# One context round of the layer-1 feed-forward layer is recorded behind the experts' last weight load instead of ahead of it

## The chip, the cores and the metric

The kernel runs on one core of a Trainium2 chip. TensorE (PE) multiplies, VectorE (DVE), ScalarE (ACT) and GpSimd (POOL) do the elementwise work, and SyncE (SP) issues nearly all loads from the chip's memory (HBM). The metric is device time in microseconds. Half a per cent of it, 13 us, is about what a measurement of this kernel can tell from no change.

## The reference, cut to what matters

Two transformer blocks run one after the other on a sequence of 256 tokens, D = 1024. The first has attention, cross attention and a mixture of 32 experts whose weights are all read. The second has two layers, and in it a second sequence, the context, runs beside the tokens with the same weights until layer 1's keys and values:

```
x = first_block(x, ...)                # ends with _hier_moe(...), 32 experts
h, hc = x, ctx                         # second_block, for layer in range(2):
h  = h  + 0.5 * mod[:, 2]  * _swiglu(_modulate(h,  ...), ffn_w_in[layer, 0], ffn_w_out[layer, 0])
hc = hc + 0.5 * modc[:, 2] * _swiglu(_modulate(hc, ...), ffn_w_in[layer, 0], ffn_w_out[layer, 0])
nx = _modulate(h, ...); nc = _modulate(hc, ...)   # then the mixer of the layer
# in layer 1 (odd) the context gives only keys and values: kc, vc = split(nc @ w_qkv[:, qdim:])
```

_swiglu has an inner width of 2816, that is 22 blocks of 128. The context does not depend on the first block at all, so its work can run at any time ahead of layer 1's attention.

## The kernel before, in words

There are two streams of recorded instructions. The fore stream is the first block and then the tokens; its tiles have names that begin with f (fraw is a loaded weight tile of 1 MB, fsph and fspl its two split parts, fps a result in PSUM). The back stream is the context; its tiles begin with b (braw is a weight tile of half a megabyte, then bsph, bspl, bps). Each product in the split form takes three matmuls of 256 columns. The fore stream has three fraw buffers (`FORE`), the back stream four braw buffers (`BACK`). A scheduler merges the two streams by priorities (`SEG`), and within a stream each engine keeps the recorded order. All loads of both streams go through one queue, SP's, in one order.

A feed-forward layer (`ffn_steps`) is a generator that yields after each of six rounds (`ROUNDS`: blocks 0 and 1, then five rounds of four). A middle round computes the gate and up products of four blocks (8 braw loads, 4 x 48 matmuls) and the down products of four (4 braw loads, 96 matmuls): 12 loads and 288 matmuls.

The experts (`moe`) are eight groups of four. A group takes 16 loads of up and gate weights (w_eg, w_eu) and 8 of down weights (w_ed), 1 MB each, and a load feeds 4 matmuls of 128x32 tiles, which the trace counts as 8; four transposes stand between the two halves, and 8 matmuls at the end (16 in the trace) add the group's result into xres (`combine`). `moe_load` is the last of these loads. A loop for rare overflow follows, and then two normalizations, which are mostly DVE work, ahead of the tokens' layer 0. The generator c1a is the context's feed-forward layer of layer 1. The table `PLAN` says where its rounds are recorded: key -1 with the context's other work, which the scheduler may put among the experts; key 0 behind the experts, with loads behind `moe_load`; keys 6 and 8 at later steps of the tokens. The lines that do it:

```
        X = K.modulated(back, c, 1, 0, 1)
        K.c1a = K.ffn_steps(back, c, X, 1, 0, K.mods_col(1, 2, 1))
        late(PLAN.get(-1, ""))
...
            if w == "r":
                next(K.c1a)
...
            if i == 0:
                K.after["sync"] = K.moe_load
                back.seg(*SEG["c1a"])
            late(PLAN[i])
```

Of the kernel before, what the change touches and what calls it, by code (L numbers as in the profile page):

```python
# [1782 lines left out]

SPILL = 4
DEFER = 0
PLAN = {-1: 'rrr', 0: 'r', 6: 'r', 8: 'raak'}
PLAN_N = 32
CUT = ((0, 9, 9, 9, 9), (0, 3, 3, 3, 3))
FORE = dict(raw=3, sph=3, spl=3, xh=1, xl=1, k1=6, k2=4, k4=6, c=16, q1=4, dg=2, ld=1, dst=6, wg=2, gc=5, c72=1, rope=1)
# [6 lines left out]
def kernel(ctx: ExitStack, tc: tile.TileContext, I, out, dbg=None, stop=None):  # L1796
# [7 lines left out]
    def context():  # L1804
# [28 lines left out]
        K.nada = CUT[1][-1]  # L1833
        late(PLAN.get(-1, ""))
        if dbg:
            dbg("hc0c", c)

    def late(what):
        c = K.cres
        for w in what:  # L1840
            if w == "r":
                next(K.c1a)
            elif w == "a":
                m = K.nada
                K.nada += 1
                for _ in K.ada(back, 1, range(m, m + 1), ("raw",)):
                    pass
            elif w == "k":
                assert next(K.c1a, None) is None and K.nada >= 5
                if dbg:  # L1850
                    dbg("hc1a", c)
                K.odd_kv(back, K.modulated(back, c, 1, 3, 1))
# [49 lines left out]
    for i in range(PLAN_N):  # L1902
        if i in PLAN:
            K.cur, K.stream = back.chain, back
# [3 lines left out]
            elif "tensor" in fore.chain:  # L1908
                K.after["tensor"] = fore.chain["tensor"]
            late(PLAN[i])  # L1910
        K.cur, K.stream = fore.chain, fore
# [157 lines left out]
```

## Time and profile before

| | us |
|---|---|
| runs | 2605.69, 2612.25, 2616.22; median 2612.25 |
| profiled execution | 2622.72 |
| its span, first to last instruction | 2620.9 |
| chain that ended last | PE 38% of the span, DVE 6%, ACT 2%, DMA 1% |

The span is cut into stretches in what follows. The experts' stage lies between about 455 and 1350 us, the tokens' layer-0 feed-forward layer between about 1400 and 1600 us. Matmuls overlap, so busy time of PE says that it has work, and the count of matmuls in a stretch says how fast it goes through it.

### The profile page before, as it was taken

How to read it: one execution, taken by the hardware profiler on the slowest of the kernel's cores; microseconds unless marked ns; L12 is line 12 of the kernel's file. 1: busy time of each engine (PE TensorE's matmuls, PEld its weight loads, DVE VectorE, ACT ScalarE, POOL GpSimd, SP SyncE). 2: the span in 40 equal slices, each digit the busy share in tenths (PEclk: the TensorE clock that was granted, in tenths of full speed). 3: DMA queues.
4: the chain of work that ended last, by engine and by line, in shares of the span. 5: the costliest groups of instructions: out<-in, count | busy, mean ns of one | idle time of the engine just before them, and what ended most of it. 6: DMA issues, size and time to landing. Idle time of an engine off the chain costs nothing. (4 is left out here: it accounts for less than half of the span.)

```text
span 2620.9 us, 48434 instructions
## 1 busy us (share of the span) xinstructions
PE 2439.5 (93%) x19032; PEld 2075.9 (79%) x19032; DVE 1448.7 (55%) x3125; ACT 1187.1 (45%) x2342; POOL 731.1 (28%) x584
## 2 busy tenths in 40 slices
PE   6999998999989999999869999999999999889998
PEld 4767998786656788778439998888899899757998
DVE  6544667224432433243128667666767876667766
ACT  4433554334433343344225555455555555465554
POOL 1000145664424465646323004232000100424000
PEclk9999999999989999999869999999999999899999
DMA  9887443998988898989874554453455455355453
GB/s 340 325 318 249 165 146 113 344 333 319 345 320 324 329 347 290 362 322 349 316 295 169 190 181 160 148 193 125 150 191 181 158 180 183 113 187 193 163 187 118
DMA packets 115238, 617.37 MB, mean 236 GB/s; under 512 B 13232, under 2 KB 14704, under 8 KB 63936
## 3 DMA queue, kind: packets, MB, share of 16 engines
q1 hardware_dynamic: 113616, 610.20, 64.1%
q0 software_dynamic: 1392, 4.06, 0.5%
q8 instruction: 150, 2.46, 0.4%
q14 instruction: 80, 0.66, 0.1%
HBM read 612.11 MB, written 2.10 MB: 234 GB/s over the span
## 5 line engine op out<-in xcount | busy, mean ns | idle before, releaser
L58 POOL TENSOR_TENSOR bspl<-braw,bsph 128x512 fp32r<-128x512 f32 x468 | 609.4, 1310 | 919.1 <-ACT bsph L58 796.8
L58 ACT ACTIVATE fsph<-fraw 128x512 fp32r<-128x512 f32 x764 | 477.7, 628 | 524.7 <-PE fps L58 438.5
L58 DVE TENSOR_TENSOR fspl<-fraw,fsph 128x512 fp32r<-128x512 f32 x712 | 500.3, 706 | 299.7 <-ACT fsph L58 292.9
L58 PE MATMUL fps<-fxh,fsph 128*128 128x256 f32 (+1 forms) x2000 | 575.7, 288 | 3.7 <-ACT fxh L58 2.4
L58 PE MATMUL fps<-fxh,fspl 128*128 128x256 f32 (+1 forms) x2000 | 574.9, 287 | 3.3 <-POOL fspl L58 2.3
L58 PE MATMUL fps<-fxl,fsph 128*128 128x256 f32 (+1 forms) x2000 | 570.1, 285 | 6.6 <-DVE fxl L58 6.6
L58 ACT ACTIVATE bsph<-braw 128x512 fp32r<-128x512 f32 x468 | 291.6, 629 | 406.8 <-PE bps L58 353.9
L58 PEld LDWEIGHTS fps<-fxh,fsph 128*128 128x128 f32 x2000 | 385.1, 193 | 11.7 <-ACT fxh L58 4.1
L58 PEld LDWEIGHTS fps<-fxl,fsph 128*128 128x128 f32 x2000 | 384.7, 192 | 9.3 <-DVE fxl L58 8.9
L58 PEld LDWEIGHTS fps<-fxh,fspl 128*128 128x128 f32 x2000 | 383.9, 192 | 8.9 <-DVE fspl L58 4.5
L58 PE MATMUL bps<-bxh,bspl 128*128 128x256 f32 x1264 | 371.1, 294 | 2.2 <-ACT fk L58 2.2
L58 PE MATMUL bps<-bxh,bsph 128*128 128x256 f32 x1264 | 367.3, 291 | 5.2 <-ACT bsph L58 1.9
L58 PE MATMUL bps<-bxl,bsph 128*128 128x256 f32 x1264 | 364.0, 288 | 1.3 <-DVE bxl L58 1.3
L58 PE MATMUL fps<-fk,fsph 128*128 128x256 f32 x1632 | 298.9, 284 | 1.8 <-ACT fk L58 1.1
L58 PEld LDWEIGHTS bps<-bxh,bspl 128*128 128x128 f32 x1264 | 246.5, 195 | 53.4 <-POOL bspl L58 33.5
L58 PE MATMUL fps<-fraw,fk 128*32 128x512 f32 (+1 forms) x1600 | 235.9, 662 | 34.4 <-DMA fraw<-in_w_eu_dram 12.5
L58 PEld LDWEIGHTS bps<-bxh,bsph 128*128 128x128 f32 x1264 | 246.6, 195 | 26.6 <-issue 10.3
L58 PEld LDWEIGHTS bps<-bxl,bsph 128*128 128x128 f32 x1264 | 246.5, 195 | 17.8 <-issue 12.6
L58 PEld LDWEIGHTS fps<-fk,fsph 128*128 128x128 f32 x1632 | 254.8, 192 | 6.1 <-DVE fk L58 2.4
L58 POOL TENSOR_TENSOR fk<-fk,fk 128x512 f32<-128x512 f32 x16 | 21.6, 1352 | 768.1 <-ACT fk L58 763.0
L58 PE MATMUL fps<-fk,fspl 128*128 128x256 f32 x816 | 231.3, 283 | 0.0
L58 DVE SCALAR_TENSOR_TENSOR bk<-bk,bps 128x256 f32<-128x256 f32 (+1 forms) x148 | 60.5, 412 | 270.4 <-ACT bk L58 268.4
(357 smaller groups left out, 3465.7 us busy)
## 6 DMA issues: line engine op xcount, KB each, us to landing
fraw<-in_ffn_in_dram SPq DMA_DIRECT2D x88, 1024.0 KB, 4.9
braw<-in_ffn_in_dram SPq DMA_DIRECT2D x132, 512.0 KB, 6.2
fraw<-in_w_eg_dram SPq DMA_DIRECT2D x66, 1024.0 KB, 7.5
fraw<-in_w_eu_dram SPq DMA_DIRECT2D x66, 1024.0 KB, 7.5
fraw<-in_w_ed_dram SPq DMA_DIRECT2D x66, 1024.0 KB, 7.4
fraw<-in_ffn_out_dram SPq DMA_DIRECT2D x44, 1024.0 KB, 4.9
braw<-in_ffn_out_dram SPq DMA_DIRECT2D x66, 512.0 KB, 6.1
braw<-in_ada_w_dram SPq DMA_DIRECT2D x59, 512.0 KB, 6.6
```

The source lines that it names most:

```text
L58: r = f(*args, **kw)
```

## The change

One number in `PLAN` moves: of the layer's six rounds, three were recorded with the context and one at key 0; now it is two and two.

```
-PLAN = {-1: 'rrr', 0: 'r', 6: 'r', 8: 'raak'}
+PLAN = {-1: 'rr', 0: 'rr', 6: 'r', 8: 'raak'}
```

SP's queue in the seventh group of experts, before: the braw rows of ffn_in and ffn_out are the context's loads, the fraw rows are the experts'.

```order
L58 DMA braw_8412<-in_ffn_out_dram 128x1024
L58 DMA braw_8484<-in_ffn_in_dram 128x1024
L58 DMA fraw_13778<-in_w_eu_dram 128x2048
L58 DMA braw_8486<-in_ffn_in_dram 128x1024
L58 DMA fraw_13798<-in_w_ed_dram 128x2048
L58 DMA braw_8561<-in_ffn_in_dram 128x1024
L58 DMA fraw_13804<-in_w_ed_dram 128x2048
L58 DMA braw_8563<-in_ffn_in_dram 128x1024
L58 DMA braw_8639<-in_ffn_in_dram 128x1024
L58 DMA fraw_13810<-in_w_ed_dram 128x2048
```

The same place of SP's queue after the change, from the same first load on.

```order
L58 DMA braw_8412<-in_ffn_out_dram 128x1024
L58 DMA fraw_13320<-in_w_eu_dram 128x2048
L58 DMA fraw_13340<-in_w_ed_dram 128x2048
L58 DMA fraw_13346<-in_w_ed_dram 128x2048
L58 DMA fraw_13352<-in_w_ed_dram 128x2048
```

Twelve braw loads are gone from here; the experts' loads follow each other, 33 of them from this place to `moe_load`, where before 24 stood behind the last braw load. Ahead of this place the queue is the same.

PE's queue in the tokens' layer-0 feed-forward layer, before, somewhat behind its start: matmuls of the tokens alone.

```order
L58 MATMUL fps_14957<-fxh_14770,fspl_14991 128x256
L58 MATMUL fps_14957<-fxh_14770,fsph_15006 128x256
L58 MATMUL fps_14957<-fxl_14771,fsph_15006 128x256
L58 MATMUL fps_14957<-fxh_14770,fspl_15007 128x256
L58 MATMUL fps_14957<-fxh_14770,fsph_15006 128x256
L58 MATMUL fps_14957<-fxl_14771,fsph_15006 128x256
```

The same matmuls of the tokens after the change, with the context's (bps) between them.

```order
L58 MATMUL bps_14294<-bxh_7679,bsph_14327 128x256
L58 MATMUL fps_14957<-fxh_14770,fsph_15006 128x256
L58 MATMUL fps_14957<-fxl_14771,fsph_15006 128x256
L58 MATMUL bps_14294<-bxl_7680,bsph_14327 128x256
L58 MATMUL bps_14294<-bxh_7679,bspl_14328 128x256
L58 MATMUL bps_14294<-bxh_7679,bsph_14327 128x256
L58 MATMUL bps_14294<-bxl_7680,bsph_14327 128x256
L58 MATMUL bps_14294<-bxh_7679,bspl_14328 128x256
L58 MATMUL fps_14957<-fxh_14770,fspl_15007 128x256
```

The context's matmuls stand in groups of mostly one to seven along the whole layer, 288 in all, and the 12 loads stand among its weight loads. What follows the last expert load directly keeps its order on PE and SP: one round fills that place as before (it is the third round now, and the fourth is the one that stands in the tokens' layer). The rounds at keys 6 and 8 stay where they were.

## Rows read from the trace of the kernel before

**Rows 1.** The page: busy time, share of the span and instructions of each engine.

```profile
PE 2439.5 (93%) x19032; PEld 2075.9 (79%) x19032; DVE 1448.7 (55%) x3125; ACT 1187.1 (45%) x2342; POOL 731.1 (28%) x584
```

**Rows 2.** Stretches: length; busy (count) PE, PEld, DVE, ACT, POOL; clock, DMA share, GB/s.

```profile
1217.00:1260.00 43.00, 43.00 (x345) 34.25 (x344) 11.93 (x26) 17.63 (x32) 28.22 (x23) 1.00 0.92 344
...
1283.00:1325.00 42.00, 25.19 (x120) 2.79 (x114) 1.52 (x3) 0.60 (x1) 0.00 (x0) 0.60 0.96 359
...
1217.00:1283.00 66.00, 66.00 (x518) 52.81 (x520) 18.96 (x40) 24.58 (x44) 39.71 (x31) 1.00 0.84 309
1283.00:1350.00 67.00, 38.94 (x188) 5.20 (x182) 3.58 (x8) 1.96 (x4) 0.00 (x0) 0.62 0.93 348
1407.00:1597.00 190.00, 190.00 (x1604) 190.00 (x1603) 132.77 (x248) 101.94 (x183) 8.16 (x7) 1.00 0.53 187
1600.00:1700.00 100.00, 93.83 (x634) 83.75 (x633) 67.68 (x148) 49.67 (x101) 32.72 (x25) 0.95 0.42 147
```

**Rows 3.** Time line of SP's queue: start, length, load issued.

```profile
1215.63 0.33 SPq L58 DMA_DIRECT2D braw<-in_ffn_out_dram  x1
...
1218.92 0.33 SPq L58 DMA_DIRECT2D fraw<-in_w_eu_dram  x1
...
1224.42 0.33 SPq L58 DMA_DIRECT2D fraw<-in_w_ed_dram  x1
...
1228.48 0.33 SPq L58 DMA_DIRECT2D fraw<-in_w_ed_dram  x1
...
1261.25 0.33 SPq L58 DMA_DIRECT2D braw<-in_ffn_out_dram  x1
1264.53 0.33 SPq L58 DMA_DIRECT2D fraw<-in_w_eg_dram  x1
...
1283.98 0.33 SPq L58 DMA_DIRECT2D fraw<-in_w_eg_dram  x1
...
1317.47 23.73 SPq L58 DMA_DIRECT2D fraw<-in_w_ed_dram  x8
```

**Rows 4.** Time line of PE: start, length, matmuls, and in brackets the idle time before.

```profile
1217.79 1.07 PE L58 MATMUL fps<-fraw,fk 128*32 128x512 f32 x8
...
1223.29 1.07 PE L58 MATMUL fps<-fraw,fk 128*32 128x512 f32 x8
...
1227.35 1.07 PE L58 MATMUL fps<-fraw,fk 128*32 128x512 f32 x8
...
1323.02 1.94 PE L58 MATMUL fps<-fraw,fk 128*32 128x512 f32 x8 [1.20 <-DMA fraw<-in_w_eu_dram]
1325.76 1.12 PE L58 MATMUL fps<-consts,fk 128*128 128x128 f32 x4 [0.81 <-DVE fc L58]
1327.56 3.64 PE L58 MATMUL fps<-fraw,fk 128*32 128x512 f32 x16 [0.69 <-ACT fk L58]
...
1350.42 3.32 PE L58 MATMUL fps<-fk,fk 128*128 128x256 f32 x8
...
1353.81 1.89 PE L58 MATMUL fps<-fk,fk 128*128 128x256 f32 x8
```

**Rows 5.** The loads: issues, KB each, median us from issue to landing.

```profile
braw<-in_ffn_in_dram SPq DMA_DIRECT2D x132, 512.0 KB, 6.2
fraw<-in_w_eg_dram SPq DMA_DIRECT2D x66, 1024.0 KB, 7.5
```

**Rows 6.** The chain that ended last, where the tokens' layer begins: start, length, what.

```profile
1407.34 72.75 PE fps L58 x613
```

**Rows 7.** PE's waits between 1590 and 1900 us: total, times, longest.

```profile
PE fps L58 <- DVE fk L58: 11.3, 6, 3.9
PE bps L58 <- DMA braw<-in_ada_w_dram: 4.1, 3, 2.8
```

## The prediction

> **What bounds the kernel now.** I read the page first: PE is busy 93% of the span [rows 1]. That is an average over stages with different limits, so I cut the span into stretches around the change [rows 2], then read the queue of loads and PE's time line there [rows 3, 4], and the chain that ended last where the round arrives [rows 6].
>
> Three stretches matter. From 1217 to 1283 us PE is busy 66.00 of 66 us: the context's matmuls stand between the experts'. The loads are near their limit too, 344 GB/s up to 1260 us, and fall to 309 GB/s over the whole stretch, because PE still works off context matmuls while the experts' loads wait for their three buffers. From 1283 to 1350 us the context's work has run out. PE is busy 38.94 of 67 us, the granted clock is at its lower level most of the time (0.62 on average), and the loads bring 348 GB/s: here the loads alone set the pace. From 1407 to 1597 us, in the tokens' layer, it is the reverse: PE is busy 190.00 of 190 us at full clock, the loads have a share of 0.53, and the chain of work that ended last runs for 72.75 us over PE without a break [rows 6]. So the change takes a round out of a stage where bytes set the end and puts it into one where matmuls set it.
>
> **What it adds.** A round is 288 matmuls of 256 columns. In the tokens' layer 1604 matmuls take 190 us [rows 2], 0.1185 us each, and PE has no idle time there that could take them: 288 x 0.1185 = 34.1 us. The upper bound is the rate of the mixed stretch of before, 518 matmuls in 66 us, 0.127 each: 36.7 us. The other engines have room in the tokens' layer: DVE is busy 132.77 and ACT 101.94 of 190 us, POOL 8.16. The round's 24 splits cost POOL about 39.71 / 31 = 1.28 us each (some 31 us, spread over the layer). Its 12 loads (512 KB each, [rows 5]) go to a queue at half its share. They cost nothing as long as this spreading holds; the price if it doesn't is a rival below. The lower bound would need idle PE time, which is another rival.
>
> **What it removes.** Twelve loads of 0.524 MB, 6.29 MB, leave the experts' stage. Its matmuls leave too, but they were what filled the waits. Three ways to price it:
>
> By bytes alone, at 344 or 348 GB/s: 18.3 or 18.1 us. This is the lower bound.
>
> By re-timing the queue [rows 3]. Both kernels are the same up to the load issued at 1215.63. The next three expert loads go out when PE frees a buffer: the weight matmuls at 1217.79, 1223.29 and 1227.35 take 1.07 us [rows 4], and the loads follow at 1218.92, 1224.42 and 1228.48. That holds after the change as well, since PE's backlog up to there is the same. Behind it PE has 34 context matmuls left (24 and 10 in its order, 4.3 us), one weight matmul and the four transposes of the seventh group; from the transposes to the next weight matmul it takes 1.8 us (1325.76 to 1327.56). So the fourth load goes out at about 1232.5, and the fifth at 1228.4 + 4.3 + 1.1 + 1.8 + 1.9 = about 1237.5. From there the loads set the pace. Before, the fifth expert load behind the last context load went out at 1283.98, and 19 more followed up to 1341.20 (the last row starts at 1317.47 and takes 23.73): 3.01 us each, which is 1.049 MB at 348 GB/s. Now 28 more follow the fifth: 1237.5 + 28 x 3.01 = 1321.8. The last load is earlier by 19.4 us, call it 19.5.
>
> By rates, if the slow end of the mixed stretch went away altogether: the two stretches move 309 x 66 + 348 x 67 = 43.7 MB in 133 us. Less 6.29 MB that is 37.4 MB, at 348 GB/s 107.5 us and at the 359 GB/s of 1283 to 1325 us 104.2 us: a gain of 25.5 to 28.8 us. This is the upper bound.
>
> I take 19.5. The slow end doesn't go away: it comes from the backlog on PE when the context's work ends, and that end is only earlier.
>
> **What else loses its cover.** The end of the seventh group had context matmuls beside it and now stands bare: the 16 matmuls that add its result take 3.32 + 1.89 = 5.2 us [rows 4]. Three buffers hold 3 x 3.01 = 9.0 us of loads meanwhile, so I cost it at nothing; without the buffers it would be 5.2 us. The 2.6 us around the transposes (1324.96 to 1327.56) hide in the same way. Directly behind the last load nothing changes: that place still holds one round, in the same order on PE and SP.
>
> More of the stage now runs at the lower clock. A load's matmuls take 1.94 us there against 1.07 at the higher one, and a load comes every 3.01 us, with PE idle before the matmuls (1.20 us before the row at 1323.02): this costs nothing. The Trainium skill's page "TensorE: Matmul & The Clock Gate", section "HAM oscillation", says that matmuls between waits for loads run at the lower clock burst after burst and that the time grows by it, which speaks against this change. The trace agrees on the clock (0.62). By the rule nine more loads at 0.87 us each would add 7.8 us and the sum would be 22.4; by the row it stays hidden.
>
> **The sum.** +34.1 - 19.5 = +14.6 us, of which nothing else hides. The profiled execution took 2622.72 us and would take 2637.3. It lies 10.5 us above the median of the runs; from the median, 2612.25, it is 2626.9, so 2627 us, slower by 0.56%. That is just over the half per cent (13 us) that a measurement here can tell from no change, so whether a measurement can tell it hangs on 2 us of the sum.
>
> **Rival 1: the experts' stage gives back more.** If without the short loads the queue ran through the slow end at full rate, the gain is 25.5 to 28.8 us and the net +5 to +9: 2617 to 2621 us, no change that can be told. For it: the 309 GB/s. Against it: the wait for buffers behind PE's backlog, which stays. The Trainium skill's page "DMA: Bandwidth & Descriptors", section "Bandwidth", has larger transfers nearer to the peak, which would help it; in the trace the mixed and the bare rate are 344 and 348 GB/s, so the size of the loads hardly tells here.
>
> **Rival 2: the tokens' layer takes it badly.** The context's matmuls stand in small groups, each waiting for a load and POOL's split, and they hold up what is queued on PE behind them. Where the trace has both streams mixed with much DVE work, from 1600 to 1700 us, PE is idle 6.2% of the time. Over 190 + 34 us that is 13.9 us: net +28.5, 2641 us. Against it: the order was made with the splits in view, and PE shows no waits from 1407 to 1597 us.
>
> **Rival 3: not slower, since the round lands in idle time.** Behind 1590 us PE waits 11.3 us for DVE and 4.1 for loads of the modulation weights [rows 7]. If the extra round pushed work into these gaps and filled all 15.4 us, the net is -0.8: 2611 us. It decides from 14.6 us filled on. Against it: the rounds at keys 6 and 8 keep their places, so no work is moved toward the gaps. That the change doesn't do what it says can be left out: both queues show the move.
>
> **How the numbers follow.** My forecast (stage gives back 17 to 22 us, round costs 33 to 37) has a chance of 0.52, with a range of its own of 2623 to 2632 us. Rival 1 has 0.28, rival 2 0.14, rival 3 0.06. The range goes from rival 1's lower end, with 2 us for the spread of the runs, to rival 2: 2615 to 2640 us. Slower by over 0.5%: most of the forecast (0.43) and of rival 2 (0.14), 0.57. Within 0.5%: the forecast's lower edge (0.09), rival 1 (0.26) and rival 3 (0.04), 0.39. Faster: 0.04.
>
> **What would show it.** After the change the experts' last load should go out 18 to 21 us earlier, around 1322 us; between about 1238 and 1330 us PE should be idle before nearly every weight matmul, with the clock near 0.6 and the loads near 348 GB/s. The tokens' layer should take about 224 us in place of 190, with PE busy all through at 0.1185 us a matmul. Wrong would be: a last load more than 24 us earlier (rival 1), PE idle or over 0.125 us a matmul in the tokens' layer (rival 2), or shorter waits behind it (rival 3).

## The result, and the profile after

| | before | after |
|---|---|---|
| median of the runs, us | 2612.25 | 2627.51 |
| ratio, 95% interval | | 1.0062, 1.0043 to 1.0081 |
| profiled execution, us | 2622.72 | 2625.72 |
| its span, us | 2620.9 | 2623.9 |

The change makes the kernel slower by 11 to 21 us (the interval times 2612.25). Its lower end lies just under the half per cent that counts here as a change.

The two profiled executions differ by only 3 us. One cause is ahead of the change: the last addition of the sixth group's result to xres ends at 1163.3 us in the profile of before and at 1156.5 in that of after, although the queues are the same up to there. In the twelve later profiles this point lies between 1153.6 and 1163.8 us. So stretches are compared here, each in its own profile, between four marks: this point, the end of the eighth group's addition, the first fk<-xres,mods operation of DVE ahead of the tokens' layer, and the same operation behind that layer. These are the marks on the time line of DVE (start, length, operation, idle time before), in the kernel before:

```profile
1162.58 0.69 DVE L58 TENSOR_TENSOR xres<-xres,fps 128x512 f32<-128x512 f32 x1 [0.17 <-PE fps L58]
...
1355.73 0.69 DVE L58 TENSOR_TENSOR xres<-xres,fps 128x512 f32<-128x512 f32 x1 [0.18 <-PE fps L58]
...
1396.45 0.86 DVE L58 SCALAR_TENSOR_TENSOR fk<-xres,mods,fps 128x256 f32<-128x256 f32 x2
...
1605.45 0.86 DVE L58 SCALAR_TENSOR_TENSOR fk<-xres,mods,fps 128x256 f32<-128x256 f32 x2
```

And in the kernel after:

```profile
1155.82 0.69 DVE L58 TENSOR_TENSOR xres<-xres,fps 128x512 f32<-128x512 f32 x1 [0.18 <-PE fps L58]
...
1326.12 0.69 DVE L58 TENSOR_TENSOR xres<-xres,fps 128x512 f32<-128x512 f32 x1 [0.17 <-PE fps L58]
...
1367.38 0.86 DVE L58 SCALAR_TENSOR_TENSOR fk<-xres,mods,fps 128x256 f32<-128x256 f32 x2
...
1611.77 0.87 DVE L58 SCALAR_TENSOR_TENSOR fk<-xres,mods,fps 128x256 f32<-128x256 f32 x2 [0.22 <-PE fps L58]
```

| us | before | after | difference |
|---|---|---|---|
| up to the end of the sixth group | 1163.3 | 1156.5 | -6.8 |
| last two groups of experts | 193.1 | 170.3 | -22.8 |
| from there to the tokens' layer | 40.0 | 40.6 | +0.6 |
| tokens' layer | 209.0 | 244.4 | +35.4 |
| behind it | 1015.4 | 1012.1 | -3.3 |

The two stretches that the change touches give -22.8 + 35.4 = +12.6 us; the medians of the runs differ by 15.3. A single profile is no finer than that: of the kernels below, five have the same instructions in the last two groups (after, e3, e5, e6, e12) and take 168.2 to 174.8 us there, and four have the same behind the layer (after, e3, e5, e6) and take 1007.3 to 1016.3 us.

The page of after has PE's busy time where it was, at the same count (it answers [rows 1]):

```profile
PE 2434.9 (93%) x19032; PEld 2067.1 (79%) x19032; DVE 1459.6 (56%) x3125; ACT 1185.8 (45%) x2342; POOL 732.9 (28%) x584
```

The stretches of after (they answer [rows 2], with the same columns):

```profile
1210.00:1240.00 30.00, 25.04 (x184) 14.59 (x186) 7.59 (x17) 5.72 (x11) 9.10 (x8) 0.88 0.81 299
1240.00:1322.00 82.00, 51.92 (x236) 9.65 (x228) 5.50 (x10) 3.22 (x6) 0.00 (x0) 0.58 0.92 344
...
1377.00:1600.00 223.00, 223.00 (x1864) 223.00 (x1863) 148.47 (x266) 115.77 (x212) 37.64 (x28) 1.00 0.53 185
1600.00:1700.00 100.00, 93.58 (x660) 83.76 (x659) 70.01 (x159) 49.37 (x101) 35.51 (x27) 0.97 0.42 144
```

From 1240 us on there is no work of the context any more: POOL, which makes its splits, is idle, PE is busy 51.92 of 82 us at a clock of 0.58, and the loads bring 344 GB/s. In the tokens' layer PE is busy 223.00 of 223 us at full clock, with 1864 matmuls.

SP's queue of after, from the load that both kernels share (it answers [rows 3]):

```profile
1208.87 0.33 SPq L58 DMA_DIRECT2D braw<-in_ffn_out_dram  x1
1212.16 0.33 SPq L58 DMA_DIRECT2D fraw<-in_w_eu_dram  x1
1217.66 0.33 SPq L58 DMA_DIRECT2D fraw<-in_w_ed_dram  x1
1221.72 0.33 SPq L58 DMA_DIRECT2D fraw<-in_w_ed_dram  x1
1225.78 0.33 SPq L58 DMA_DIRECT2D fraw<-in_w_ed_dram  x1
1229.36 2.83 SPq L58 DMA_DIRECT2D fraw<-in_w_ed_dram  x3
1236.28 0.33 SPq L58 DMA_DIRECT2D fraw<-in_w_ed_dram  x1
...
1291.70 21.73 SPq L58 DMA_DIRECT2D fraw<-in_w_ed_dram  x8
```

From the shared load to the last expert load it is 1313.43 - 1208.87 = 104.6 us; before it was 125.6 [rows 3]. The last load goes out 21.0 us earlier by the queue's own measure.

PE's time line of after, in the bare stretch (it answers [rows 4]):

```profile
1272.67 1.93 PE L58 MATMUL fps<-fraw,fk 128*32 128x512 f32 x8 [3.12 <-DMA fraw<-in_w_eu_dram]
1275.14 1.93 PE L58 MATMUL fps<-fraw,fk 128*32 128x512 f32 x8 [0.53 <-DMA fraw<-in_w_eg_dram]
1277.60 1.94 PE L58 MATMUL fps<-fraw,fk 128*32 128x512 f32 x8 [0.53 <-DMA fraw<-in_w_eu_dram]
```

PE takes 1.93 us for a load's matmuls and then waits for the next load: the slow matmuls still have time left.

In the kernel before, the chain that ended last runs over the tokens' matmuls alone from 1407.34 us on; the 72.75 us of [rows 6] are only what the view shows up to 1480 us, and the piece is 184.5 us long. After the change it is broken into short pieces, between which it passes from one stream's matmuls to the other's. Its shares by line, 1370 to 1620 us, of after:

```profile
by line: PE fps L58 77.6%; PE bps L58 19.8%; DVE fc L58 2.0%; DVE bk L58 0.3%; DVE fk L58 0.1%; issue 0.1%
```

PE's waits behind the tokens' layer, 1600 to 1920 us (they answer [rows 7], in a stretch that is 10 us longer), are about what they were:

```profile
PE fps L58 <- DVE fk L58: 11.8, 7, 4.5
PE bps L58 <- DMA braw<-in_ada_w_dram: 3.9, 3, 2.5
```

### The profile page after: what moved, and what is told of

The parts are those of the page before. It is cut to its first block, busy times and chain, and to the rows that moved or that the text cites. A ratio compares the mean times of both kernels' runs of the same rounds, so it can differ in the third digit from the quotient of the medians.

```text
span 2623.9 us, 48427 instructions
## 1 busy us (share of the span) xinstructions
PE 2434.9 (93%) x19032; PEld 2067.1 (79%) x19032; DVE 1459.6 (56%) x3125; ACT 1185.8 (45%) x2342; POOL 732.9 (28%) x584
## 4 chain that ended last, share of the span: by engine, by line
PE 40%; DVE 6%; ACT 2%; DMA 1%; issue 1%; POOL 0%; DVEq 0%; ACTq 0%; SPq 0%; POOLq 0%
PE fps L58 35%; PE bps L58 5%; DVE fc L58 2%; DVE fk L58 1%; DVE fspl L58 1%; DVE xres L58 1%; ACT bk L58 1%; ACT fsph L58 1%; DVE fxl L58 0%; DVE bk L58 0%; ACT fk L58 0%; DMA fraw<-in_o_out_dram 0%; DMA fraw<-in_ffn_in_dram 0%; DMA braw<-in_ada_w_dram 0%; DMA fraw<-in_o_q_dram 0%
## 5 line engine op out<-in xcount | busy, mean ns | idle before, releaser
L58 DVE TENSOR_TENSOR fspl<-fraw,fsph 128x512 fp32r<-128x512 f32 x712 | 506.4, 714 | 314.9 <-ACT fsph L58 307.7
L58 PEld LDWEIGHTS bps<-bxh,bspl 128*128 128x128 f32 x1264 | 244.5, 193 | 48.0 <-POOL bspl L58 30.2
L58 PE MATMUL fps<-fraw,fk 128*32 128x512 f32 (+1 forms) x1600 | 241.4, 676 | 40.8 <-DMA fraw<-in_w_ed_dram 14.3
L58 PEld LDWEIGHTS bps<-bxl,bsph 128*128 128x128 f32 x1264 | 244.4, 193 | 19.0 <-issue 13.9
L58 PE MATMUL bps<-bk,bsph 128*128 128x256 f32 x1056 | 199.1, 284 | 0.3 <-DVE bk L58 0.3
```

Source lines behind the costliest of these rows:

```text
L58: r = f(*args, **kw)
```

## The experiments

Each kernel was timed beside the kernel before; ratios are to that. Stretches are cut at the marks above, in us.

| kernel | ratio, interval | last two groups | to the layer | layer | behind it |
|---|---|---|---|---|---|
| before | 1 | 193.1 | 40.0 | 209.0 | 1015.4 |
| after | 1.0062, 1.0043 to 1.0081 | 170.3 | 40.6 | 244.4 | 1012.1 |
| e1_no_loads | 0.9939, 0.9920 to 0.9959 | 174.0 | 41.0 | 209.1 | 1012.6 |
| e2_few_matmuls | 0.9944, 0.9926 to 0.9962 | 179.2 | 41.7 | 209.0 | 1010.7 |
| e3_after_few_matmuls | 0.9985, 0.9968 to 1.0001 | 168.2 | 40.5 | 223.4 | 1016.3 |
| e4_two_moved | 1.0076, 1.0056 to 1.0096 | 151.9 | 41.4 | 246.4 | 1042.3 |
| e5_round_gone | 0.9884, 0.9861 to 0.9907 | 170.2 | 41.4 | 211.5 | 1007.3 |
| e6_only_matmuls | 1.0053, 1.0034 to 1.0072 | 174.8 | 39.2 | 244.3 | 1015.5 |
| e7_one_pulled | 1.0048, 1.0031 to 1.0065 | 209.7 | 41.4 | 204.4 | 1012.7 |
| e8_all_ahead | 1.0003, 0.9989 to 1.0016 | 209.0 | 23.8 | 203.8 | 1020.3 |
| e9_spread | 0.9983, 0.9970 to 0.9996 | 186.7 | 40.7 | 208.6 | 1012.3 |
| e10_spread2 | 0.9979, 0.9968 to 0.9991 | 189.5 | 40.1 | 209.0 | 1012.2 |
| e11_spread3 | 0.9975, 0.9963 to 0.9987 | 185.5 | 42.5 | 208.9 | 1010.7 |
| e12_at_mixer | 1.0023, 1.0011 to 1.0036 | 172.4 | 41.4 | 209.1 | 1040.7 |

**Bytes or matmuls in the experts' stage.** The kernel before, with one half of its third round taken out at a time. In e1 the round's 12 loads are left out and its splits read a constant tile (`THIN = (2,)`). In e2 272 of its 288 matmuls are left out (`LITE = (2,)`).

```
-            raw = self.pair(S, w_in[l, j, f])
+            raw = [self.cst[:, :1024]] * 2 if lean(f + 1, THIN) else self.pair(S, w_in[l, j, f])
...
+                if lite:
+                    if k == 0:
+                        self.mm(out, h[:, :128], X.h[k], True, True)
...
+                    continue
```

> The kernel before, with the 12 loads of the context's third round left out: its splits read a constant tile instead, and its 288 matmuls stay among the experts (so the context's result is not the reference's). If bytes set the end of the experts' stage (my theory), the time falls by as much as taking the whole round away gave back, 18 to 22 us, to about 2592. If PE sets it (the stage is 66.00 of 66 us busy), the matmuls are all still there and the time stays within 4 us of before.

> The kernel before, with 272 of the third round's 288 matmuls left out (one matmul is kept for each product), all 12 loads and 24 splits kept. If bytes set the end of the stage, the queue carries the same 43.7 MB and gains only the slow end behind PE's backlog: 2 to 8 us. If PE sets it, 272 x 0.127 = 34.5 us go and the time falls by 30 us or more.

The runs became faster by 16 us without the loads, somewhat less than the 18 to 22 expected if bytes set the end, and by 15 us without the matmuls, which is neither the 2 to 8 of bytes nor the 30 or more of PE. So neither limit holds alone. The stage gave back 19.1 us without the loads and 13.9 without the matmuls. Both together, which is what the change takes away, gave 22.8 and not 33. The stretches (columns as in [rows 2]) say why; first e1, then e2:

```profile
1210.00:1240.00 30.00, 30.00 (x243) 23.57 (x242) 9.65 (x20) 12.06 (x21) 19.53 (x17) 1.00 0.69 246
```

```profile
1210.00:1270.00 60.00, 45.12 (x260) 22.21 (x259) 20.35 (x41) 23.20 (x44) 38.63 (x31) 0.80 0.95 369
1270.00:1330.00 60.00, 38.40 (x165) 4.89 (x166) 2.74 (x6) 1.79 (x3) 0.00 (x0) 0.55 0.94 346
```

Without the round's loads PE stays busy all through these 30 us and the queue falls to 246 GB/s: it waits for PE. Without its matmuls PE has idle time in the mixed stretch too, and the queue carries 369 GB/s there, where before it carried 344 and then less [rows 2]. So in the mixed stretch of before PE held the loads, and behind it the loads held PE. Either half of the round shortens the stage, and they share part of what they save: the five kernels without the round there gave back 18.3 to 24.9 us.

**What costs time in the tokens' layer.** Three versions of the kernel after. e3 leaves out 272 of the moved round's 288 matmuls, by the edit of e2 with `LITE = (3,)`. e5 leaves out its loads and splits as well. e6 keeps all 288 matmuls but feeds them with tiles that are there already, without loads and splits; this one is told apart from e5 by a constant `FEW`:

```
+            if lite:
+                for k in range(a, a + m):
+                    w = X.h[(k + 1) % 8][:, :128]
+                    if FEW and k == 0:
+                        self.mm(out, w, X.h[k], True, True)
...
+                        self.mm3(out, w, w, X.h[k], X.l[k], k == 0, k == nk - 1)
+                continue
```

> The kernel after the change, with 272 of the 288 matmuls of the round that now stands in the tokens' layer left out, its loads and splits kept. If the round costs its matmuls at the pace of that layer, 272 x 0.1185 = 32 to 35 us go against the kernel after, which is 17 to 21 us under the kernel before. If half the cost is waits for splits and loads (rival 2), no more than 25 us go and the time is within 10 us of before.

> The kernel after the change, with the moved round reduced to its elementwise work: no loads, no splits, one matmul for each product instead of 12 or 24. What is left of the change is what the experts' stage gives back. My theory: the tokens' layer is back at about 196 us and the time is 19 to 24 us under before, about 2591. If the 15.6 us that the layer kept in the run with few matmuls come from the longer chain of products and not from the splits, they stay and the time is near that run, 2608.

> The kernel after the change, with all 288 matmuls of the moved round kept, but taken from values already there: its 12 loads and 24 splits are left out. If the matmuls set the cost of the round in the tokens' layer, the layer stays at 229 to 233 us and the time within 4 us of the kernel after. If the splits on POOL and ACT set it, the time falls by the 15 us that they cost in the run with few matmuls.

With the matmuls alone (e6) the layer takes 244.3 us, as in the kernel after with everything (244.4): the loads and splits add nothing, and the time is that of the kernel after, as expected. (The expectations of e5 and e6 count the layer between other, closer cuts: 196 and 229 to 233 us.) These are the two marks of e6:

```profile
1367.71 0.86 DVE L58 SCALAR_TENSOR_TENSOR fk<-xres,mods,fps 128x256 f32<-128x256 f32 x2
...
1612.05 0.87 DVE L58 SCALAR_TENSOR_TENSOR fk<-xres,mods,fps 128x256 f32<-128x256 f32 x2 [0.22 <-PE fps L58]
```

With neither (e5) it takes 211.5. But with the loads and splits and few matmuls (e3) it takes 223.4, 14.4 more than before, which the 16 matmuls that are left can't explain. So e3 did not fall by the 17 to 21 us under the kernel before that its theory gave (its runs are 4 to 6 us under it, which is what its rival had), and e5 puts the difference down to the loads and splits, as its own theory had it.

The time of e5 fell by 24 to 36 us against before, more than the 19 to 24 expected. In its profile 8.1 us of this stand behind the layer, where nothing was taken out; why is open. By the runs alone e5 saved as much as e1 and e2 together. That the two halves share what they save rests on the profiles of the stage, and on the runs of after and e12: they are 15.3 and 7.0 us over before, with 35.4 and 25.3 us more elsewhere, which leaves 20 and 18 us given back.

The rows of e3 between 1372 and 1573 us: operations of DVE and POOL with their mean duration, and PE's wait (total, times, longest):

```profile
L58 DVE TENSOR_TENSOR fspl<-fraw,fsph 128x512 fp32r<-128x512 f32 x131 | 100.0, 766 | 43.8 <-ACT fsph L58 43.7
...
L58 DVE TENSOR_TENSOR bk<-bk,bk 128x256 fp32r<-128x256 f32 x4 | 5.7, 1418 | 0.0
```

```profile
L58 POOL TENSOR_TENSOR bspl<-braw,bsph 128x512 fp32r<-128x512 f32 x26 | 40.5, 1589 | 4.3 <-ACT bsph L58 4.2
```

```profile
PE fps L58 <- DVE fspl L58: 5.5, 5, 1.4
```

The same operations in e6, 1378 to 1600 us, where POOL has 2 such splits and not 26:

```profile
L58 DVE TENSOR_TENSOR fspl<-fraw,fsph 128x512 fp32r<-128x512 f32 x131 | 91.6, 701 | 73.7 <-ACT fsph L58 73.3
...
L58 DVE TENSOR_TENSOR bk<-bk,bk 128x256 fp32r<-128x256 f32 x4 | 1.7, 419 | 0.0
```

While POOL splits, DVE's work stretches; PE, which with so few matmuls of the context is ahead, waits for the tokens' splits. This shows in part of the time only: over the whole layer e3 takes 11.9 us longer than e5, of which 6.9 are more idle time of PE and 5.0 longer busy time for as many matmuls, which the rows do not explain. Waits for the moved round's loads play no part; ACT, which reads them first, waits 0.2 us for one. In the kernel after, between 1377 and 1600 us and with the same 26 splits of POOL, DVE's splits are stretched too:

```profile
L58 DVE TENSOR_TENSOR fspl<-fraw,fsph 128x512 fp32r<-128x512 f32 x131 | 96.9, 742 | 66.0 <-ACT fsph L58 65.6
```

But there the round's matmuls give DVE the time, PE waits for nothing, and the cost is that of the matmuls alone.

**Other places for a round.** Only `PLAN` is changed, from the kernel before; the added lines are those of e4, e7, e8 and e12, in this order.

```
-PLAN = {-1: 'rrr', 0: 'r', 6: 'r', 8: 'raak'}
+PLAN = {-1: 'r', 0: 'rrr', 6: 'r', 8: 'raak'}
+PLAN = {-1: 'rrrr', 0: 'r', 8: 'raak'}
+PLAN = {-1: 'rrrr', 6: 'r', 8: 'raak'}
+PLAN = {-1: 'rr', 0: 'r', 6: 'rr', 8: 'raak'}
```

> The same move once more: one round ahead of the experts' end, three at key 0. If each round gives back its bytes (18 to 21 us) and costs its matmuls (34 to 37 us), the second costs as much as the first: +30 us against before, 2642. If PE sets the pace of the stage where the second round is taken from, it gives back up to 36 us and the time stays near the kernel after, +13 to +18.

> The other direction, from a later place: the rounds are rrrr ahead of the experts' end, r at key 0, none at key 6. By the prices so far (a round in the experts' stage costs 19 to 24 us, a round from key 6 on costs about 30) the time falls by 6 to 11 us against before, to about 2604. If the round at key 6 only fills idle time there, the time rises by 10 us or more.

> The round of key 0 ahead of the experts' end as well: rrrr there, none at key 0. The place directly behind the last load, which a round fills in both kernels, is then empty; DVE's normalizations set its length (47 of 54 us of PE busy there before). If that round is free where it is, taking it away gains no more than 10 us while the experts' stage pays 19 to 24: +10 to +20 us against before. If it costs its matmuls there as in the tokens' layer, the time falls by about 10.

> The kernel before with the third round's place given up as in the change, but the round that takes up the slack recorded at key 6, behind the tokens' layer 0, in place of key 0, so that two rounds stand there. Theory (the first round at key 6 fills idle time and costs 7 us, the second finds PE busy and costs what the third moved round cost behind the tokens' layer, 27 to 30 us): the experts' stage gives back 20 to 23 us, the tokens' layer stays at 209 us, the rest of the span grows by 25 to 30 us, and the time is 2 to 10 us over the kernel before, ratio 1.001 to 1.004. Rival (key 6 takes a second round as cheaply as the first): the rest grows by 7 to 10 us and the time falls by 11 to 15 us, ratio 0.9943 to 0.996.

e4 took 20 to 22 us more than before, between its two forecasts of 30 and 13 to 18. e7 took 13 us more, as its second forecast had it: the round at key 6 fills idle time. e8 came out level with before, where +10 to +20 or -10 was expected. Read together, the stretches price a round by its place, each against the one profile of before:

| place of the round | us | from |
|---|---|---|
| experts' last two groups: the third one taken out | 18 to 25 | after 22.8, e3 24.9, e5 22.9, e6 18.3, e12 20.7 |
| ... the second one taken out as well | 18.4 | 170.3 - 151.9, e4 |
| ... a fourth one added | 16 to 17 | e7, e8 |
| behind the last load, the first one there | 21.5 | e8: 16.2 ahead of the layer and 5.2 in it |
| tokens' layer | 35 | after, e6 |
| key 6, the first one there | 5 to 7 | e7: 4.6 in the layer and 2.7 behind it, which is within the spread there |
| key 6, a second one (in e4 it comes from the round in front) | 25 to 30 | e12 25.3; e4 26.9 against before, 30.2 against after |

The first round at key 6 fills mostly idle time of PE, and the one behind the last load does in part; the next one at either place finds it filled. e12's theory held: the stage gave back 20.7, the part behind the layer grew by 25.3, and the ratio was within the 1.001 to 1.004 expected. Its rival, a second cheap round at key 6, fell. The cheap place at key 6 is taken in the kernel before, and the places left cost more than the stage gives back, so none of these moves of a whole round wins. e8 saves 21.5 for 16 and is still only at 1.0003, since the part behind the layer came out 4.9 us longer; its 1020.3 us lie outside the 1007.3 to 1016.3 of the four kernels above, and what makes it longer was not tried.

**Spreading the round thinly.** If PE holds the loads first and the loads hold PE afterwards, mixing the same round evenly should save time without moving it out. The third round (in e10 also the second) is recorded in five pieces between given weight loads of the last groups; matmuls, loads and splits stay the same. A key of `PLACES` is a group, counted from 0, and a step in it; the three lines are those of e9, e10 and e11. `PLAN` loses one `r` of key -1 for each round that is spread.

```
+PLACES = {(6, 8): 1, (7, 0): 1, (7, 3): 1, (7, 6): 1, (7, 8): 1}
+PLACES = {(5, 8): 1, (6, 0): 1, (6, 3): 1, (6, 5): 1, (6, 8): 1, (6, 10): 1, (7, 1): 1, (7, 3): 1, (7, 5): 1, (7, 7): 1}
+PLACES = {(6, 3): 1, (6, 9): 1, (7, 2): 1, (7, 5): 1, (7, 9): 1}
...
+    def place(grp, k):
+        for _ in range(PLACES.get((grp, k), 0)):
+            K.after["sync"] = fore.chain["sync"]
+            K.cur, K.stream = back.chain, back
+            next(K.c1a)
...
```

> The kernel before with its third round kept ahead of the experts' end, but recorded in five pieces (four gate-up products, one down) between the weight loads of the seventh and eighth expert groups, in place of all at once with the context's other work. Matmuls, loads and splits are the same. Theory (in the mixed stretch PE's backlog holds the loads' queue, behind it the loads hold PE, and the two limits are paid one after the other): mixed thinly, the queue runs on at about 350 GB/s and PE has no bare stretch, so the stage from the seventh combine but one to the last combine takes 175 to 185 us in place of 193.1, the tokens' layer stays at 209 us, and the time is 8 to 18 us below the kernel before, ratio 0.993 to 0.997. Rival (the bytes of the stage alone set its length, wherever the matmuls stand): stage 190 to 195 us, within 4 us of before, ratio 0.9985 to 1.0015. Second rival (small pieces stall PE on a load and a split in order, ahead of the experts' matmuls): stage over 197 us, ratio 1.002 or more.

> As the run before it, but with the second and the third round both recorded in pieces, over the loads of the sixth to eighth expert groups. Theory of limits paid one after the other: at least as much as from one round in pieces, 10 to 22 us below the kernel before, ratio 0.9915 to 0.996, with clock and loads even over the stage (0.9 and about 345 GB/s). Rival (bytes alone): within 4 us of before. Second rival (pieces stall PE in order): slower than before, more so than with one round in pieces.

> The third round in five pieces again, with other places: none directly at the start of the eighth group, where the first such run had the pieces' matmuls next to those that add the seventh group's result and the experts' loads waited 8 us for a buffer. Theory (a piece costs when it stands next to other work of PE that already uses up the buffers' 9 us): the waits for a buffer of that size go, the last two groups take 181 to 185 us in place of 193.1 before and 186.7 in the first such run, and the time is 8 to 12 us below the kernel before, ratio 0.9954 to 0.997. Rival (what is left is the cost of the bytes and of waits for splits, wherever the pieces stand): the same as the first such run, ratio 0.9975 to 0.9990.

All three are faster than the kernel before, e11 at 0.9975, with intervals that leave out 1, but by 4 to 7 us and not by the 8 to 22 expected; that is less than the half per cent that counts here as a change. The stage of e9 took 186.7 us, between the theory's 175 to 185 and the rival's 190 to 195; e10, which should have saved at least as much, took 189.5, with the first of its ten pieces ahead of the stage, and its runs can't be told from those of e9. So the direction held and the size was wrong. e11's own theory was that what is lost are waits next to the seventh group's addition. Its ratio is at the edge of its rival's range, with an interval that reaches into the theory's, but waits of 8 us for a buffer did not go: they stand at other places. SP's queue and the stretch between in e11:

```profile
1274.18 0.33 SPq L58 DMA_DIRECT2D fraw<-in_w_eg_dram  x1
1281.93 0.33 SPq L58 DMA_DIRECT2D fraw<-in_w_eu_dram  x1
```

```profile
1274.00:1282.00 8.00, 5.85 (x27) 3.55 (x24) 0.00 (x0) 2.41 (x4) 4.96 (x4) 0.57 1.01 419
```

A piece begins here. PE is idle for part of the time, waits for ACT's and POOL's splits of the piece's fresh loads (2.6 and 1.9 us in all in the last two groups of e11), and works its matmuls at a clock of 0.57 behind that idle time. Meanwhile no expert load can go out. But those already issued land at 419 GB/s, so the row shows PE's waits and its clock, and no gap in the bytes. The last two groups as a whole, first before, then e9 (columns as in [rows 2]):

```profile
1163.00:1356.00 193.00, 164.94 (x1155) 105.64 (x1148) 38.62 (x78) 50.55 (x92) 79.53 (x62) 0.86 0.90 331
```

```profile
1159.00:1346.00 187.00, 160.77 (x1156) 110.19 (x1153) 40.62 (x78) 50.33 (x92) 79.45 (x62) 0.93 0.91 340
```

The same matmuls, and a queue at 340 GB/s in place of 331. What keeps it from the 369 of e2 is not shown. Splits and clock are a guess from these rows; a version with the pieces' loads and splits made earlier was not tried.

## Why the prediction was right

The predicted 2627 us and the measured 2627.51 agree, the sign too, and both terms were sized by the mechanism that the runs show. That the agreement is so close is luck: both terms came out larger than predicted, by 1.3 and 3.3 us, which leaves +12.6 by the stretches against +14.6 predicted and +15.3 in the runs, and the interval of the runs is 10 us wide.

**What bounds each stretch.** For the tokens' layer and the bare stretch this held. For the mixed stretch "the loads are near their limit too, 344 GB/s" was wrong: e2 has 369 GB/s at the same place when PE has less to do. There PE was the bound. The 72.75 us of the chain without a break understated it: the piece is 184.5 us long, which makes the same point more strongly.

**The round in the tokens' layer: +34.1 predicted, +35.4 measured,** within its bound of 36.7. The rate is 223.00 / 1864 = 0.1196 us a matmul against 0.1185 taken from the rows of before. e6 shows that matmuls alone are the whole of it.

**What the experts' stage gives back: -19.5 predicted, -22.8 in the profile of after,** -18.3 to -24.9 with the other kernels that lack the round there (mean of the five 21.9). The mechanism, PE's backlog that ends earlier and loads that set the pace from then on, is what the queue shows: the second to fourth expert loads behind the shared one went out 8.8, 12.9 and 16.9 us after it, as worked out. The size was off at the hand-over. The eighth was due 21.9 + 3 x 3.01 = 30.9 us behind the shared load and came after 27.4, since three loads left together at 1229.36: two of the experts' loads lay ready behind the transposes, and PE worked the matmuls of both off in 1.92 us, from 1228.23 on, where the prediction had one. Of the 3.5 us the later loads gave back 1.9, at 3.09 us each and not 3.01 (77.15 us for 25). Another 1.8 us came behind the last load, where 12.7 us pass from its issue to the end's addition against 14.5 before (1326.12 - 1313.43 and 1355.73 - 1341.20 on DVE's and SP's time lines). The last load went out 21.0 us earlier, within the 18 to 21 named as the sign. The by-rates bound of 25.5 to 28.8 took the slow end of the mixed stretch for one that might vanish; the measured mean is between the two ways of working it out.

**What loses its cover.** Costed at nothing, and it was little. PE waits for loads behind the seventh group's end, so the 5.2 us of its addition do not show in full. But the queue has a dip there: two expert loads go out 5.7 us apart (1248.22 and 1253.87), and from 1246 to 1256 us the loads bring 272 GB/s in place of the 344 of the whole bare stretch. That is an estimated 2 us, about what the later loads gave back. The slower matmuls at the lower clock (1.93 us) also stayed hidden behind waits for loads. The Trainium skill's page "TensorE: Matmul & The Clock Gate", section "HAM oscillation", would have the time grow by such bursts, to a sum of 22.4 us as the prediction worked out. The trace agrees on the clock, 0.58, and not on the time, since the loads set the pace here.

**The rivals.** Rival 1 (the stage gives back 25.5 us or more) was reached by no kernel; e3's 24.9 came near. Rival 2 (waits for splits in the tokens' layer) names a mechanism that exists, 14.4 us in e3, but the round's own matmuls hide it. Its 28.5 did not come. Rival 3 (the round fills the waits behind the layer) did not happen: 11.8 and 3.9 us of waits stand where there were 11.3 and 4.1.

## What to carry to other kernels

Price a piece of work by the place where it would stand, not by its length: the same round was worth 5 to 7 us in mostly idle time, about 20 beside the weight loads and 35 among back-to-back matmuls. When PE holds the first half of a stage and the loads hold the second, the averages over the stage (331 GB/s, PE busy 165 of 193 us) hide it; mixing the work thinly gave 4 to 7 us back here, less than hoped. And when two profiles differ less than the runs do, compare stretch by stretch from a point that the change can't reach.

## What the runs showed that was not expected

- DVE is slower while POOL splits: the tokens' split on DVE took 701 ns on average with 2 splits of POOL beside it (e6), and with 26 it took 742 in the kernel after and 766 in e3. The context's product bk<-bk,bk, of which there are only four, took 419, 416 and 1418 ns. POOL's split took 1349 ns in the kernel after and 1589 in e3; what it takes with DVE idle no run shows. DVE's operations with one input from PSUM did not stretch: bk<-bk,bps took 419 ns in e6 and 414 in e3. The Trainium skill's page "SBUF — State Buffer", section "Who interferes with whom", says that a DVE instruction with two inputs from SBUF contends with a GpSimd instruction that reads SBUF, and that one with at most one such input, outside DVE's 2-port modes, does not. The trace agrees with both.
- The queue of loads can go faster than its bare rate of 344 to 348 GB/s: 369 over 60 us in e2, and 419 over 8 us in e11, in both cases with the context's buffers in flight beside the three of the experts. The Trainium skill's page "DMA: Bandwidth & Descriptors", section "Bandwidth", gives 341 GB/s for transfers of 1 MB and 425 for those of 16 MB, measured with GpSimd as the issuer. The rates named here, with SP as the issuer and loads of 0.5 and 1 MB, lie between the two; what holds the bare stretch at 348 was not tried.
- Leaving out the 12 loads alone shortened the stage by 19.1 us, leaving out 272 matmuls alone by 13.9, and leaving out the whole round by 22.8 and not by 33.
- Executions of the same instructions differ by up to 10 us ahead of the point at which the change begins (1153.6 to 1163.8 us).
